# A transformer block on one core: context path at two steps per expert, and three VectorE passes spread over ScalarE and GpSimd

## Chip, core and metric

The kernel runs on one core of a Trainium2 chip. TensorE (PE; its weight loads are PEld), VectorE (DVE), ScalarE (ACT) and GpSimd (POOL) each run their own instructions strictly in order; SyncE (SP) issues the DMAs, also in order; a gather (indirect DMA) is issued by GpSimd. The metric is the device time of one execution in microseconds (us); lower is better.

## Reference, cut to what matters

512 tokens, width 1024, one batch. The first block's attention makes h; then a mixture of 32 experts (two per token), an embedding branch gated by h, and a second block of two attention layers, which also attend to a context of 256 tokens.

```python
def hier_moe(x, w_rg, w_re, w1, w3, w2):
    ...
    def expert_block(args):
        xb, e = args
        hdn = jax.nn.silu(xb @ w1[e]) * (xb @ w3[e])
        return hdn @ w2[e]
    ...
# end of first_block
h = h + hier_moe(rms_norm(h, g_ffn[i]), w_rg[i], w_re[i], w1[i], w3[i], w2[i])
h = h + rms_norm(p[i] @ w_ple[i], g_ple[i]) * jax.nn.sigmoid(rms_norm(h, g_plg[i]) @ w_plg[i])
```

The context goes through the first attention layer of the second block by itself (`yc`, `ctx = ctx + gate_c * yc`) and then gives keys and values (`kc`, `vc`) to the second layer. Nothing of it depends on the experts.

## The kernel before

The program is written out in Python as one long list of instructions. A scheduler puts them in order for each engine: by the order in which the program writes them, moved where its own timing says that an engine would stand idle. So where a filler's instructions stand in the program moves them, but does not fix them.

The part that matters is the loop `for e in range(E)` over the 32 experts (numbered from 0). An expert takes 12 weight tiles `we` of 512 KB (`w1` and `w3` four each, from a ring of 11 tiles `W`; `w2` four, from a ring `Y`), 32 products of `w1` and `w3` (each two instructions, `d<-we,exT`), four transpositions (`t<-ident,eth`), 8 products of `w2` (two instructions each, `d<-we,eth`), and writes its rows to DRAM (`y_d<-ey`). Pairs of experts share a gather `xg` and its transpositions.

Between the experts the loop runs steps of a generator `filler`: first `ctx_path` (56 steps: the keys and values of the context's first layer, four times a projection and two attention pairs, the output product in two halves with 96 products 512 wide `s<-...,cot`, the second layer's input product `mla_in`, and four blocks `mla_kv` whose results are stored as `kvc_d`), then `ple` (a step that loads and transposes the embedding input `px`, and one step for each of four chunks of 128 tokens: 12 products 512 wide, then `pu` is scaled by its norm `r` and by the gain `gple`). `due(e)` says how many steps have to be done after expert e: `CTX_RATE` times e - 1, rounded down. A dense product is done in three fp32r parts (`whi,Xhi`, `wlo,Xhi`, `whi,Xlo`), which need `raw` split into `whi` on ScalarE and `wlo` on GpSimd or VectorE.

Ahead of expert 24 (`OVF_AT`) stands a loop `overflow()` over experts with more than 64 tokens, whose count is a register: all engines meet there. In the profiled execution it has no turn (no instruction touches its tiles `wp`).

Behind the experts every chunk c of 128 tokens gathers its two rows `yk` from `y_d`, adds them to `h2` with the weights `wts`, norms the sum (`row_norm`: squares on ScalarE, then `rsq`: `rs_m` on VectorE, a power on GpSimd), scales it (`xp`), transposes it (`make_X`), and multiplies it by `w_plg` in two blocks of 512 columns, 24 products for a chunk and block (`b_plg`; its tiles are `h2`, `xp`, `pth`). Here it is called the gate product. Nothing of the second block can begin before it.

Of the kernel before, what the change touches and what calls it, by code (L numbers as in the profile page):

```python
# [16 lines left out]
AF = mybir.ActivationFunctionType  # L17
OP = mybir.AluOpType
# [23 lines left out]
PREP_LEAD = 2  # L42
D_PRE, GQA_PRE, MLA_PRE = 5, 14, 34
MOD_FROM, EARLY = 8, 30
CTX_FROM, CTX_RATE, CTX_FINE = 2, 1.65, 3
PREL, OVF_AT, PLE_AT, PLE_FIRST = 2, 24, 29, 2
MLA_ST, MLA_FIRST, MLA_MIX = 2, 8, (1, 3)


# [33 lines left out]
def block_kernel(ctx: ExitStack, tc: tile.TileContext, I, out, dbg=None):  # L83
    nc = tc.nc
# [81 lines left out]
    def share(**us):  # L166

        e = min(us, key=lambda e: held[e] + us[e])
        busy(**{e: us[e]})
        return eng[e]  # L170

    def kcols(ap):
        return math.prod(ap.shape[1:]) / 1000

    def copy(o, i, on=("act", "dve")):

        us = dict(act=0.06 + 0.83 * kcols(o), dve=0.07 + 1.04 * kcols(o))
        e = share(**{n: us[n] for n in on})
        (e.copy if e is nc.scalar else e.tensor_copy)(o, i)  # L179
# [224 lines left out]
    def row_norm(x, n):  # L404

        ssq = SM([P, 1], "ssq1", bufs=4)
        nc.scalar.activation(junk[:, :n], x, AF.Square, accum_out=ssq)
        return rsq(ssq, 1, 1.0 / n)

    def scaled(y, x, r, g):  # L410

        nc.vector.scalar_tensor_tensor(y, x, r, g, op0=OP.mult, op1=OP.mult)
# [591 lines left out]
    for c in range(NC4):  # L1004
        r = row_norm(xs[c], D)
# [466 lines left out]
    xp, gp = [], []  # L1472

    def ple_load():
        if not xp:
            gp.append(Y([P, D], name="gple"))
            gp.append(load_row(gp[0], I["g_ple"], D))
            for c in range(NC4):
                x = T2([P, 256], name="px")
                load(x, I["p"][rows(c), :])  # L1480
                xp.append(x)


    def ple():
        wpv = I["w_ple"].rearrange("(p c) n -> p c n", c=2)
        blks = [Dense(wpv, 2, [(b * 512, 512)]).load().split() for b in range(2)]
        ple_load()
        gp[1]()
        Xp = make_Xs(xp, 2)
        yield  # L1490
        for b, d in enumerate(blks):
            d.X = Xp
            d.evac = lambda c, ps, b=b: copy(us[c][b], ps)
        for c in range(NC4):
            us.append([(K3 if c < 3 else T2)([P, 512], name="pu") for _ in range(2)])
            ssq = SM([P, 2], "ussq")
            for b in range(2):
                blks[b].chunk(c)
                nc.scalar.activation(junk[:, :512], us[c][b], AF.Square, accum_out=ssq[:, b:b + 1])
            nc.vector.tensor_tensor(ssq[:, 0:1], ssq[:, 0:1], ssq[:, 1:2], op=OP.add)  # L1500
            r = rsq(ssq[:, 0:1], 1, 1.0 / D)
            nc.vector.tensor_scalar(r, r, 0.5, None, op0=OP.mult)
            for b in range(2):
                scaled(us[c][b], us[c][b], r, gp[0][:, b * 512:(b + 1) * 512])
            yield

    def due(e):
# [2 lines left out]
    us, paid = [], [0]  # L1510
# [19 lines left out]
    _, wts, yidx, oidx, ovf_e, novf = res  # L1530
# [35 lines left out]
    yks = []  # L1566
# [10 lines left out]
    for c in range(NC4):  # L1577
        h = h2[c]
        if c + 1 < NC4:
            fetch(c + 1)  # L1580
        for k in range(2):
            nc.vector.scalar_tensor_tensor(h, yks[2 * c + k], wts[:, k, c:c + 1], h, op0=OP.mult, op1=OP.add)
        dbg(f"h2_{c}", h)
        r = row_norm(h, D)
        x = Y([P, D], name="xp")
        scaled(x, h, r, gplg)
        Xt.append(make_X(x, 8))
        next(filler, None)
# [356 lines left out]
```

## Time and profile before

| | us |
|---|---|
| median of 3 runs | 1904.56 (1900.89 to 1907.15) |
| the profiled execution: time | 1905.35 |
| its span | 1903.6 |
| TensorE busy | 1682.1 |
| VectorE busy | 932.2 |
| ScalarE busy | 740.0 |
| GpSimd busy | 613.3 |

The span runs from the first to the last instruction of the program; 1.75 us lie around it. Busy times overlap, and a busy TensorE counts the whole latency of a product, so that products which wait for each other look busy. The experts take from 431 to 1052 us of the span, and move 224.6 MB there.

### The profile page before, as it was taken

The numbers are of one execution on the slowest core, as the hardware profiler recorded it, in microseconds if no ns is written. First come the engines' busy times: TensorE is split into PE (matmuls) and PEld (weight loads), VectorE is DVE, ScalarE is ACT, GpSimd is POOL, SyncE is SP. The second block draws the span as 40 slices with busy tenths as digits, with TensorE's granted clock in tenths as the row PEclk, the third lists the DMA queues.
The fourth block names the chain that finished last, engine by engine and source line by source line (L and its number), as shares of the span: only waits on it lengthen the run. The fifth ranks groups of instructions, "written<-read, shape, count | busy, mean of one in ns | idle before, by whom it ended". The sixth has DMA issues, their size and how long they took to land. (4 is left out here: it accounts for less than half of the span.)

```text
span 1903.6 us, 28348 instructions
## 1 busy us (share of the span) xinstructions
PE 1682.1 (88%) x10457; PEld 1202.6 (63%) x10457; DVE 932.2 (49%) x2017; ACT 740.0 (39%) x1620; POOL 613.3 (32%) x697
## 2 busy tenths in 40 slices
PE   7998778969999889899897799898989989879989
PEld 6787555655655545555553478775657877757757
DVE  5765547452232222221233866575652756776641
ACT  5245347412222212221222444355662544656660
POOL 4862113212212212122112434533223545453231
PEclk9999788989999999999898899999999989999999
DMA  8441697778999998998999533100023535331031
GB/s 244 155 173 62 201 283 228 246 259 311 380 409 397 368 380 325 369 322 290 357 409 380 196 105 117 51 1 1 1 89 125 153 108 165 115 98 45 23 133 45
DMA packets 190078, 386.38 MB, mean 203 GB/s; under 512 B 27768, under 2 KB 85720, under 8 KB 189936
## 3 DMA queue, kind: packets, MB, share of 16 engines
q1 hardware_dynamic: 186480, 376.13, 56.2%
q0 software_dynamic: 3456, 8.39, 1.4%
q8 instruction: 84, 1.38, 0.3%
q14 instruction: 58, 0.48, 0.1%
HBM read 350.96 MB, written 39.17 MB: 205 GB/s over the span
## 5 line engine op out<-in xcount | busy, mean ns | idle before, releaser
L150 PE MATMUL d<-we,exT 128*64 128x256 f32 x2048 | 254.9, 393 | 13.2 <-DMA we<-in_w 10.4
L150 PE MATMUL d<-whi,Xhi 128*128 128x512 f32 (+2 forms) x560 | 219.3, 394 | 8.1 <-DVE gsg L588 3.4
L150 PE MATMUL d<-wlo,Xhi 128*128 128x512 f32 (+2 forms) x560 | 218.5, 390 | 3.6 <-POOL wlo L251 3.6
L150 PE MATMUL d<-whi,Xlo 128*128 128x512 f32 (+2 forms) x560 | 218.9, 391 | 2.5 <-DVE Xlo L182 2.4
L251 POOL TENSOR_TENSOR wlo<-raw,whi 128x1024 fp32r<-128x1024 f32 (+2 forms) x71 | 172.5, 2449 | 149.8 <-ACT whi L242 73.8
L150 PEld LDWEIGHTS d<-we,exT 128*64 128x64 f32 x2048 | 149.1, 141 | 102.0 <-issue 22.7
L514 DVE TENSOR_REDUCE ast<-s 128x1 f32<-128x768 f32 (+1 forms) x160 | 135.3, 848 | 99.7 <-PE s L150 97.9
L242 ACT CAST whi<-raw 128x1024 fp32r<-128x1024 f32 (+2 forms) x130 | 131.5, 1019 | 119.6 <-PE d L150 69.2
L516 ACT ACTIVATE pr<-s,ast 128x768 f32<-128x768 f32 (+1 forms) x160 | 131.2, 821 | 59.2 <-DVE ast L514 55.6
L153 PE MATMUL t<-ident,pr 128*128 128x128 f32 x832 | 124.8, 281 | 14.2 <-DVE PT L179 7.0
L150 PE MATMUL s<-stk 128*128 128x256 f32 x448 | 120.4, 355 | 18.7 <-ACT pr L516 14.8
L248 POOL TENSOR_TENSOR wlo<-raw,whi 128x512 fp32r<-128x512 f32 (+2 forms) x69 | 82.1, 1218 | 145.3 <-ACT whi L242 72.0
L150 PEld LDWEIGHTS d<-whi,Xhi 128*128 128x128 f32 x560 | 107.9, 193 | 31.2 <-DVE gsg L588 3.6
L150 PE MATMUL d<-we,eth 128*64 128x512 f32 x512 | 121.8, 606 | 5.2 <-DVE eth L1424 5.2
L150 PEld LDWEIGHTS d<-wlo,Xhi 128*128 128x128 f32 x560 | 108.0, 193 | 24.3 <-POOL wlo L251 4.6
L150 PEld LDWEIGHTS d<-whi,Xlo 128*128 128x128 f32 x560 | 107.8, 192 | 23.5 <-DVE Xlo L182 3.6
L150 PE MATMUL d<-whi,ot 128*128 128x512 f32 x384 | 120.1, 392 | 1.4 <-DVE rT L1283 0.9
L153 PEld LDWEIGHTS t<-ident,pr 128*128 128x128 f32 x832 | 95.7, 143 | 38.3 <-DVE PT L179 11.0
L150 PEld LDWEIGHTS s<-stk 128*128 128x128 f32 x448 | 70.5, 195 | 35.1 <-ACT pr L516 23.6
L1448 POOL DMA_INDIRECT xg<-xn_d,gidx x16 | 16.7, 1041 | 216.8 <-PE t L153 123.4
L1416 DVE SCALAR_TENSOR_TENSOR eth<-eth,d 128x256 f32<-128x256 f32 x32 | 13.5, 421 | 148.4 <-ACT eth L1415 148.4
L150 PEld LDWEIGHTS d<-whi,ot 128*128 128x128 f32 x384 | 71.9, 188 | 18.7 <-issue 1.8
(475 smaller groups left out, 3188.9 us busy)
## 6 DMA issues: line engine op xcount, KB each, us to landing
we<-in_w SPq DMA_DIRECT2D x378, 512.0 KB
raw<-in_l_w_mod SPq DMA_DIRECT2D x48, 512.0 KB
raw<-in_l_w_in SPq DMA_DIRECT2D x64, 256.0 KB
raw<-in_w_in SPq DMA_DIRECT2D x24, 512.0 KB
raw<-in_l_w_out SPq DMA_DIRECT2D x24, 512.0 KB
raw<-in_l_w_in SPq DMA_DIRECT2D x16, 512.0 KB
y_d<-ey SPq DMA_DIRECT2D x64, 128.0 KB
bias<-bias SPq DMA_DIRECT2D x48, 128.0 KB
```

The costliest lines, as they stand in the source:

```text
L150: nc.tensor.matmul(o, l, r, start=start, stop=stop)
L153: nc.tensor.transpose(o, x, identr if x.dtype == F32R else ident)
L242: nc.scalar.copy(t, src)
L248: e.tensor_tensor(t, src[:, k], hi[k].bitcast(F32), op=OP.subtract)
L251: e.tensor_tensor(t, src, whole.bitcast(F32), op=OP.subtract)
L514: nc.vector.tensor_reduce(st[:, h:h + 1], ps, op=OP.max, axis=AX.X, negate=True)
L516: nc.scalar.activation(p, ps, AF.Exp, bias=st[:, h:h + 1], accum_out=sums[:, c, h:h + 1])
L1416: nc.vector.scalar_tensor_tensor(th[:, 256:], th[:, :256], 1.0, ps[:, :256], op0=OP.add, op1=OP.mult)
L1448: nc.gpsimd.indirect_dma_start(out=x, out_offset=None, in_=src, in_offset=bass.IndirectOffsetOnAxis(ap=idx, axis=0), bounds_check=src.shap ...
```

## The change

```diff
-CTX_FROM, CTX_RATE, CTX_FINE = 2, 1.65, 3
-PREL, OVF_AT, PLE_AT, PLE_FIRST = 2, 24, 29, 2
+CTX_FROM, CTX_RATE, CTX_FINE = 2, 2.0, 3
+PREL, OVF_AT, PLE_AT, PLE_FIRST = 2, 24, 28, 2
...
         for b, d in enumerate(blks):
             d.X = Xp
-            d.evac = lambda c, ps, b=b: copy(us[c][b], ps)
+            d.evac = lambda c, ps, b=b: nc.scalar.copy(us[c][b], ps)
...
             for b in range(2):
-                scaled(us[c][b], us[c][b], r, gp[0][:, b * 512:(b + 1) * 512])
+                nc.gpsimd.tensor_tensor(us[c][b], us[c][b], gp[0][:, b * 512:(b + 1) * 512], op=OP.mult)
+                nc.scalar.activation(us[c][b], us[c][b], AF.Copy, scale=r)
...
-        for k in range(2):
-            nc.vector.scalar_tensor_tensor(h, yks[2 * c + k], wts[:, k, c:c + 1], h, op0=OP.mult, op1=OP.add)
+        y0, y1 = yks[2 * c:2 * c + 2]
+        nc.scalar.activation(y0, y0, AF.Copy, scale=wts[:, 0, c:c + 1])
+        nc.gpsimd.tensor_tensor(h, h, y0, op=OP.add)
+        nc.vector.scalar_tensor_tensor(h, y1, wts[:, 1, c:c + 1], h, op0=OP.mult, op1=OP.add)
```

With the rate 2.0 the 56 steps of the context path are due after expert 29, and four more steps (the embedding's first and three of its chunks) after expert 31; with 1.65 there are 49 steps due after expert 31, and the rest stands behind the loop. `PLE_AT` loads the embedding's input one expert earlier. The scaling of `pu` becomes a product on GpSimd and a scaling on ScalarE; the first of the two rows of a token is scaled on ScalarE and added on GpSimd, the second stays on VectorE.

What this does to the order is shown at three places. First SyncE's queue around the overflow loop (`raw<-in_l_w_kv_b` are the weights of `mla_kv`, `raw<-in_w_ple` those of the embedding, `mrow` and `g` small rows). Before, behind the loop:

```order
L129 DMA y_d<-ey 64x512
L129 DMA we<-in_w 128x1024 x16
L129 DMA raw<-in_l_w_kv_b 128x2x512
L129 DMA y_d<-ey 64x512 x2
L129 DMA mrow<-mod_118 1x1024
L129 DMA raw<-in_l_w_kv_b 128x2x512 x2
L129 DMA mrow<-mod_118 1x1024
L129 DMA raw<-in_l_w_kv_b 128x2x512
```

And after the change, in front of the loop (whose first instruction is `COMPARE_AND_BRANCH`):

```order
L129 DMA we<-in_w 128x1024 x6
L129 DMA g_7594<-in_R 1x896
L129 DMA we<-in_w 128x1024 x12
L129 DMA raw<-in_w_ple 128x2x512
L129 DMA y_d<-ey 64x512 x2
L129 DMA we<-in_w 128x1024 x8
L129 DMA y_d<-ey 64x512 x2
L129 DMA we<-in_w 128x1024 x11
L129 DMA raw<-in_w_ple 128x2x512
L129 DMA we<-in_w 128x1024
L129 DMA y_d<-ey 64x512
L1455 COMPARE_AND_BRANCH
```

Four loads for `mla_kv` and both for the embedding have moved from behind the loop to before it.

Second the end of SyncE's queue for the experts, as a piece of the difference (`raw<-in_w_plg` are the weights of the gate product, `h` the tiles `h2`):

```order
+L129 DMA kvc_d<-cvc 128x2x256
+L129 DMA raw<-in_w_plg 128x2x512
+L129 DMA we<-in_w 128x1024
+L129 DMA kvc_d<-cyk 128x2x256
+L129 DMA we<-in_w 128x1024 x6
+L129 DMA y_d<-ey 64x512 x2
+L129 DMA we<-in_w 128x1024 x4
 L129 DMA gplg<-in_g_plg 1x1024
-L129 DMA we<-in_w 128x1024 x3
+L129 DMA h_9180<-h_d 128x1024
+L129 DMA we<-in_w 128x1024
```

The last weight tile, `we` at the end of this piece, now stands behind a load of `w_plg` (three more stand further ahead, not shown) and one of `h2`; before, all loads of `w_plg` and `h2` stood behind the last `we`, as did six of the eight stores `kvc_d`, which now all stand ahead of it.

Third the last part of the experts' tail on GpSimd, from the first gathers `yk`. Before:

```order
L1448 DMA yk<-y_d,yidx 128x1024 x4
L741 TENSOR_TENSOR cyk<-cyk,g_8252 128x256 x2
L196 TENSOR_TENSOR rs_y<-rs_m,mhalf 128x1
L251 TENSOR_TENSOR wlo<-raw,whi 128x1024 x2
L196 TENSOR_TENSOR rs_y<-rs_m,mhalf 128x1 x2
L741 TENSOR_TENSOR cyk<-cyk,g_8252 128x256 x2
L196 TENSOR_TENSOR rs_y<-rs_m,mhalf 128x1
L1448 DMA yk<-y_d,yidx 128x1024 x2
L196 TENSOR_TENSOR rs_y<-rs_m,mhalf 128x1 x2
L1448 DMA yk<-y_d,yidx 128x1024 x2
L196 TENSOR_TENSOR rs_y<-rs_m,mhalf 128x1 x2
```

After:

```order
L1448 DMA yk<-y_d,yidx 128x1024 x4
L1584 TENSOR_TENSOR h_9180<-h_9180,yk 128x1024
L1584 TENSOR_TENSOR h_9181<-h_9181,yk 128x1024
L196 TENSOR_TENSOR rs_y<-rs_m,mhalf 128x1
L1504 TENSOR_TENSOR pu<-pu,gple 128x512
L1448 DMA yk<-y_d,yidx 128x1024 x2
L1504 TENSOR_TENSOR pu<-pu,gple 128x512
L196 TENSOR_TENSOR rs_y<-rs_m,mhalf 128x1 x2
L1448 DMA yk<-y_d,yidx 128x1024 x2
L1584 TENSOR_TENSOR h_9182<-h_9182,yk 128x1024
L1584 TENSOR_TENSOR h_9183<-h_9183,yk 128x1024
L196 TENSOR_TENSOR rs_y<-rs_m,mhalf 128x1 x2
```

The two splittings `wlo` and the context's last `cyk` are gone from here, and four additions and two products stand in their place. On VectorE, behind the last expert's copy, after the change (`h_9180` to `h_9183` are the four chunks, `t_9432` is the second chunk's transposition):

```order
L412 SCALAR_TENSOR_TENSOR xp<-h_9181,rs_y,gplg 128x1024
L1585 SCALAR_TENSOR_TENSOR h_9182<-yk,wts,h_9182 128x1024
L1585 SCALAR_TENSOR_TENSOR h_9183<-yk,wts,h_9183 128x1024
L194 TENSOR_SCALAR rs_m<-ssq_9457 128x1
L1604 SCALAR_TENSOR_TENSOR pth<-pth,pu 128x512
L182 TENSOR_TENSOR Xlo<-t_9432,Xhi 128x512
L182 TENSOR_TENSOR Xlo<-t_9439,Xhi 128x512
L412 SCALAR_TENSOR_TENSOR xp<-h_9182,rs_y,gplg 128x1024
```

The second chunk's `Xlo`, which the gate product of that chunk needs, stands behind the sums of the third and the fourth chunk.

## Rows read from the trace of the kernel before

**Rows 1.** Windows at experts 4, 13, 24: engines' busy us, clock, DMA share, GB/s

```profile
496.00:670.00 174.00, 161.67 (x1082) 97.77 (x1081) 46.08 (x131) 44.34 (x108) 41.16 (x48) 1.00 1.01 389
670.00:893.00 223.00, 200.43 (x1297) 118.28 (x1296) 49.90 (x127) 49.14 (x119) 46.67 (x51) 0.96 0.92 340
893.00:1052.00 159.00, 136.96 (x837) 75.57 (x836) 47.84 (x117) 34.69 (x73) 29.73 (x26) 0.90 0.98 374
1052.00:1101.00 49.00, 35.09 (x150) 26.27 (x150) 43.81 (x88) 25.18 (x57) 23.35 (x22) 0.90 0.47 156
```

**Rows 2.** Timeline, TensorE: one expert's parts, then two dense products

```profile
877.47 3.67 PE L150 MATMUL d<-we,exT 128*64 128x256 f32 x32
893.96 3.65 PE L150 MATMUL d<-we,eth 128*64 128x512 f32 x16
1030.10 0.66 PE L153 MATMUL t<-ident,eth 128*64 128x128 f32 x4
1110.01 0.39 PE L150 MATMUL d<-whi,Xlo 128*128 128x512 f32 x1
1110.24 0.39 PE L150 MATMUL d<-whi,Xhi 128*128 128x512 f32 x1
```

**Rows 3.** Waits of SyncE's queue in 520:640, 640:880, 960:1040: total, times, longest

```profile
SPq L129 <- DMA we<-in_w: 57.1, 68, 1.5
SPq L129 <- PE d L150: 88.4, 88, 4.5
SPq L129 <- DMA we<-in_w: 41.6, 50, 1.4
```

**Rows 4.** Timeline, SyncE: at the overflow loop; the last weights' issue

```profile
883.82 9.75 SPq L129 DMA_DIRECT2D y_d<-ey  x2
893.63 15.07 SPq L129 DMA_DIRECT2D we<-in_w  x16
1025.11 1.87 SPq L129 DMA_DIRECT2D we<-in_w  x3
```

**Rows 5.** Timeline, TensorE: from the last expert to the gate product

```profile
1037.11 2.76 PE L150 MATMUL d<-we,exT 128*64 128x256 f32 x24
1045.69 5.84 PE L150 MATMUL d<-we,eth 128*64 128x512 f32 x16
1080.54 1.94 PE L153 MATMUL t<-ident,xp 128*128 128x128 f32 x8 [9.49 <-DVE rs_y L1502]
1100.10 0.71 PE L153 MATMUL t<-ident,xp 128*128 128x128 f32 x4 [0.89 <-DVE Xlo L182]
```

**Rows 6.** Timeline, 1056 to 1081: GpSimd (two rows), VectorE (three rows)

```profile
1056.56 1.04 POOL L1448 DMA_INDIRECT yk<-y_d,yidx  x1 [9.49 <-PE s L150]
1069.68 5.76 POOL L251 TENSOR_TENSOR wlo<-raw,whi 128x1024 fp32r<-128x1024 f32 x2 [6.00 <-PE d L150]
1066.18 0.15 DVE L201 SCALAR_TENSOR_TENSOR rs_u<-rs_m,rs_y 128x8 f32<-128x8 f32 x1
1070.97 2.19 DVE L203 SCALAR_TENSOR_TENSOR rs_y<-rs_u,rs_y 128x8 f32<-128x8 f32 x1
1079.13 1.27 DVE L412 SCALAR_TENSOR_TENSOR xp<-h,rs_y,gplg 128x1024 f32<-128x1024 f32 x1
```

**Rows 7.** Tile yk: the sums on VectorE, and the gathers' landing

```profile
L1582 DVE SCALAR_TENSOR_TENSOR h<-yk,wts,h x8: 1269/1278/1285, 1063.1 to 1092.5; 128x1024 f32<-128x1024 f32 x8
DMA to landing us min/median/max: 4.5/6.7/7.1
```

**Rows 8.** Groups by form (busy us, mean ns): GpSimd's splittings

```profile
L251 POOL TENSOR_TENSOR wlo<-raw,whi 128x1024 fp32r<-128x1024 f32 x65 | 162.5, 2519 | 136.9 <-PE d L150 67.3 <-ACT whi L242 60.9 <-DMA raw<-in_w_out 6.6
L248 POOL TENSOR_TENSOR wlo<-raw,whi 128x512 fp32r<-128x512 f32 x54 | 68.4, 1297 | 119.5 <-ACT whi L242 62.6 <-issue 32.3 <-DMA we<-in_w 16.2
```

**Rows 9.** Tile pu: VectorE's scaling, ScalarE's copies (ns min/median/max)

```profile
L412 DVE SCALAR_TENSOR_TENSOR pu<-pu,rs_y,gple x8: 739/748/1291, 1068.3 to 1086.6; 128x512 f32<-128x512 f32 x8
L179 ACT COPY pu<-d x4: 564/576/589, 1058.6 to 1072.1; 128x512 f32<-128x512 f32 x4
```

## The prediction

> **What bounds the kernel now.** I read the windows first, cut where the first product of an expert begins. From expert 4 to 13 (496 to 670 us) the DMA engines are full (share 1.01); from 13 to 24 they fall to 0.92 and 340 GB/s; from 24 to the end of the last expert they are at 0.98; then, up to the steady part of the gate product, at 0.47, and TensorE is busy for 35 of 49 us [rows 1]. In this last stretch VectorE has 43.8 of 49 us: there it is the full engine. The waits of SyncE's queue say the same: between 520 and 640 us it waits for earlier weights to land (57 us), between 640 and 880 mostly for TensorE to give tiles back (88 us), between 960 and 1040 for the landing again (42 us) [rows 3]. So the experts are bound by the DMAs, then by TensorE, then by the DMAs.
>
> Busy TensorE counts latency, so I price its work from runs of products. 32 instructions of w1 and w3 take 3.67 us, so 7.3 for the 64; w2 takes 3.65; the four transpositions 0.66 [rows 2]; with half a pair's gathered rows (about 0.5, an estimate from these four) an expert is 12.2 us. A dense product 512 wide is issued every 0.23 us [rows 2]. With half of this for 256 wide, and 0.13 (estimated) for a transposition, I counted the filler's work in both orders: what stands ahead of the experts 4, 13, the overflow loop, and the last w2 is 14, 62, 114, 133 us before, and 17, 63, 128, 146 us after.
>
> **The experts up to the overflow loop.** 14 us of TensorE work and 4.2 MB of loads (four for mla_kv, two for the embedding, two weight tiles) move from behind the loop to before it. Up to expert 13 the two counts agree within 3 us, so I take no difference there. From 13 to the loop TensorE has 11 x 12.2 + 52 = 186 us of work in 223, that is 83%; after the change 11 x 12.2 + 65 = 199. The 4.2 MB have room: at the 389 GB/s of the stretch before, the 223 us would carry 11 MB more than at 340 [rows 1]. What 14 us of work cost depends on whether the idle 17% can be used. From 4 to 13 the same engine did 9 x 12.2 + 48 = 158 us in 174, or 91%; at that share 199 us take 219, 4 us less than now. If every idle moment stays, the loop comes 14 us later. I take +5, the middle of -4 and +14: the earlier stretch is the nearest row, but this one holds the coarser steps (the output product's halves, 11 us each).
>
> **From the loop to the last weights.** SyncE stands at the loop (9.75 us for two stores), begins again at 893.6, and issues the last weight tile at about 1027 [rows 4]: 133 us. In the order before, 52.3 MB go out in between; after, 52.6 MB: four loads of w_plg, one of h2 and six stores of the context come ahead of the last weights, and what moved before the loop makes room for them. At 389 GB/s 52.6 MB take 135 us, at the 374 of the whole stretch 141 [rows 1]; this stretch already ran at 393. So it can hardly give more than the few us in which the second layer's context products keep TensorE from freeing tiles, and these now lie before the loop. I take -3, between 0 and -5.
>
> **The last expert.** Its w1 and w3 end at 1039.9; its w2 runs from 1045.7 to 1051.5 [rows 5], 5.84 us where 3.65 are normal [rows 2]: the granted clock is 0.90 on the mean of this stretch [rows 1], so part of it is at 1.2 instead of 2.4 GHz. After the change two of the embedding's chunks (24 products, 5.5 us) stand between them in place of the gain's broadcast. They fill the wait and keep TensorE at work, but lie in front of w2. I take -1 (0 to -2).
>
> **The tail.** Times from here on count from the end of w2 (1051.5). Before, the first gather starts at +5.1 [rows 6], the first sum at +11.6 [rows 7], the first xp only at +27.6 [rows 6], its transposition at +29.1, after 9.5 us of idle, and TensorE is steady from +49 on, with two chunks done and the third begun (50 dense products lie between) [rows 5].
>
> The arithmetic that leaves VectorE here: four sums of 1.28 [rows 7], eight scalings of 0.75 and four copies, which take ScalarE 0.58 [rows 9] and VectorE hardly less, some 13 us in all, most of the scalings and copies now within the experts. GpSimd gets four additions of 128x1024 and eight products of 128x512; the trace has none of these, and the nearest rows are its splittings of the same shape with two inputs, 2.5 and 1.3 us [rows 8]. ScalarE's scaling of 1024 columns I put at 1.1, twice a copy of 512 [rows 9]. So a chunk's sum, once 2.6 us on one engine, becomes 1.1 + 2.5 + 1.3 on three. I walk along the new order: first rows at +10 (a landing takes 4.5 to 7.1 us [rows 7]), scaled at +11, added at +13.6, second row at +15; the next chunk's rows land at about +14.5, its addition ends at +18; the first chunk's power stands behind it on GpSimd, +18.7; xp ends at +21, and the gate product may begin at +23.5 instead of +31.
>
> But the second chunk's Xlo now stands on VectorE behind the sums of the third and fourth. Their gathers stand on GpSimd behind two products and three powers: the last first-row gather goes out at about +25, lands at +32, is scaled and added by +35; VectorE's sum ends at +36.5, Xlo at +38. TensorE is steady from +38, with one chunk done and the second begun: behind the old state by one chunk (24 x 0.23 = 5.5) and 12 transpositions (1.6). 49 - 38 - 7 is a gain of 4 us (0 to 6).
>
> One row speaks against this part. A VectorE operation on 8 columns took 2.19 us, begun while GpSimd was in two splittings of 5.76 [rows 6]; one of that shape just before it took 0.15 [rows 6]. I take 1.2 us off the walk for one such stop of xp behind a product of pu; this is in the 4. The Trainium skill (SBUF — State Buffer, section "SBUF: two separate sides") says that GpSimd and a VectorE operation with two SBUF inputs share a port pair that one of them holds for a whole instruction. By that rule, the trace agrees: that operation has two such inputs. Were each of the six GpSimd operations to stop VectorE for its full length (4 x 2.5 + 2 x 1.3 = 12.6), the gain would be gone; most of the time VectorE waits for these very results, so I leave that to a rival.
>
> **Sum.** +5 - 3 - 1 - 4 = -3 us on the profiled execution's 1905.4, so 1902.4; the median stands 0.8 lower. I predict 1902. Behind the gate product both orders differ only by a few exchanged transpositions and products (some 70 of 2,400 rows on TensorE), for which I allow 2 us. About 0.3% (5.7 us) is what a measurement of this kernel can tell from no change.
>
> **Rivals.** *The idle time before the loop is used* (30%): the stretch from 13 to 24 runs as densely as the one before it. For it: the DMA share there is lower only because TensorE holds tiles [rows 3], and the new order spreads the output product's halves. Against it: TensorE's latency chains are as many as before. The loop comes no later (0), the rest gives -4, -1, -5: 1895.
> *The moved work is paid in full* (20%, slower): before the loop TensorE is what SyncE waits for [rows 3], so 14 us of work push the loop back by 14; behind it the DMAs are full and give nothing, -0 - 1 - 3: +10, 1915. It decides from a loop more than 11 us later, if the tail gives no more than 4.
> *The tail is not shortened* (12%): the gathers' landing and the port hold the sums, as worked out; +5 - 3 - 1 + 0: 1906.
> The change could fail to do what it says only in the tail's order, which is read above.
>
> **Chances.** My forecast has 38%: 30 within 0.3%, 7 faster, 1 slower. The first rival (30) is faster, the second (20) slower; of the third, 10 are within, 2 slower. Faster 0.37, same 0.40, slower 0.23. The range takes in the first rival with a denser tail (1890) and the second but for its far end (1914); the forecast's own is 1897 to 1908.
>
> **What would show it.** The last issue ahead of the overflow loop and SyncE's restart: near 899 if I am right, 907 or more for the second rival, 893 or less for the first. From there to the last weight tile 128 to 133 us. The first transposition of xp at 22 to 24 us behind the last w2 instead of 29, and a wait of TensorE for Xlo in the second chunk. An addition on GpSimd much above 2.5 us, or a VectorE operation of over 2 us beside one, speaks for the third rival. I am wrong if the loop's place moves by more than 10 us either way, or if the first stretch, where I took no difference, is not the same.

## The result and the profile after

The changed kernel takes 1936.08 us (median of 4 runs, 1930.59 to 1940.74), the kernel before 1902.72 us beside it (4 runs, 1899.51 to 1907.15). The ratio is 1.0164, 95% interval 1.0138 to 1.0191: 33 us slower, outside my range, which ended at 1914. (One run of a kernel below, 2013.5 us at a granted clock of 0.815 where its nine others took 1909 to 1921, is left out.) The profiled execution of the changed kernel has a span of 1930.9 us, 27.3 more than that of before; the terms below are made against this one.

The windows of the changed kernel, cut again where experts 4, 13 and 24 begin and where the last w2 ends (same columns as [rows 1]):

```profile
496.00:670.00 174.00, 160.99 (x1075) 100.51 (x1073) 48.27 (x137) 43.21 (x112) 37.33 (x46) 0.95 0.97 364
670.00:930.00 260.00, 223.89 (x1390) 138.48 (x1388) 66.42 (x174) 62.79 (x144) 58.06 (x62) 0.90 0.86 324
930.00:1079.00 149.00, 130.77 (x794) 69.84 (x791) 34.80 (x101) 35.34 (x77) 26.87 (x23) 0.93 0.97 378
1079.00:1130.00 51.00, 23.38 (x87) 17.83 (x85) 17.36 (x25) 19.80 (x32) 31.25 (x21) 0.67 0.38 129
```

Beside [rows 1]: the first stretch is as long as it was (174 us), the second 37 us longer (260 for 223) with emptier DMAs (324 GB/s for 340) and a lower granted clock (0.90 for 0.96), the third 10 us shorter (149 for 159). In the last, VectorE has gone from 43.8 of 49 us to 17.4 of 51, and nothing was won by it. SyncE's queue at the overflow loop and at the last weight tile, which answers to [rows 4]:

```profile
916.01 12.33 SPq L129 DMA_DIRECT2D y_d<-ey  x2
...
929.03 3.71 SPq L129 DMA_DIRECT2D we<-in_w  x6
...
1056.53 1.11 SPq L129 DMA_DIRECT2D we<-in_w  x1
```

The queue stands at the loop at 916 instead of 884 and goes on with weights at 929.0 instead of 893.6: 35.4 us later. From there to the end of the last weight issue it needs 128.6 us, where it was about 133. TensorE's timeline from the last w2 on, which answers to [rows 5]:

```profile
1074.99 3.65 PE L150 MATMUL d<-we,eth 128*64 128x512 f32 x16
...
1081.20 0.39 PE L150 MATMUL d<-whi,Xlo 128*128 128x512 f32 x1
1102.12 1.97 PE L153 MATMUL t<-ident,xp 128*128 128x128 f32 x8 [20.53 <-DVE xp L412]
...
1117.42 0.80 PE L150 MATMUL d<-whi,Xhi 128*128 128x512 f32 x1 [4.90 <-ACT Xhi L390]
...
1120.44 0.80 PE L150 MATMUL d<-whi,Xlo 128*128 128x512 f32 x1 [1.79 <-DVE Xlo L182]
```

The last w2 now takes 3.65 us instead of 5.84 and ends at 1078.6. The first transposition of xp comes 23.5 us later (29.0 before; I had 22 to 24), but after 20.5 us of idle in one piece, and the second chunk waits for its Xhi and Xlo as foreseen: TensorE is steady from +42, where I had +38.

### The profile page after: what moved, and what is told of

The parts are those of the page before. It is cut to its first block, busy times and chain, and to the rows that moved or that the text cites. A ratio compares the mean times of both kernels' runs of the same rounds, so it can differ in the third digit from the quotient of the medians.

```text
span 1930.9 us, 28369 instructions
## 1 busy us (share of the span) xinstructions
PE 1686.3 (87%) x10457; PEld 1213.0 (63%) x10457; DVE 918.3 (48%) x1999; ACT 753.7 (39%) x1638; POOL 633.4 (33%) x709
## 5 line engine op out<-in xcount | busy, mean ns | idle before, releaser
L150 PE MATMUL d<-whi,Xhi 128*128 128x512 f32 (+2 forms) x560 | 219.6, 394 | 11.1 <-ACT Xhi L390 5.6
L150 PE MATMUL s<-whi,Xhi 128*128 128x512 f32 (+2 forms) x192 | 76.4, 401 | 5.6 <-ACT pr L516 4.2
```

The costliest lines, as they stand in the source:

```text
L150: nc.tensor.matmul(o, l, r, start=start, stop=stop)
```

## What the experiments share

All times by stretch below are read from the timelines in the same way: from the start of the span to the first product of expert 13, from there to the first of expert 24, from there to the end of the last w2, and the rest. They and the spans are those of the profiled execution; the medians are over all runs of a kernel, and a span is about 2 us shorter than its own execution's time. Ratios are against runs of the kernel before that were made beside each (medians 1901.8 to 1903.5). The first lines are the two kernels.

```
                                to e13   13-24   24-w2 end   behind    span    median
before                           670.1   222.9     158.5     852.0   1903.6   1902.7
changed                          670.4   259.3     148.9     852.3   1930.9   1936.1
rate alone                       674.3   259.6     149.8     841.2   1924.9   1926.1
sharing alone, rate 1.65         669.9   223.2     156.9     870.3   1920.3   1925.3
rate 2.0, four experts later     654.7   249.9     156.0     848.5   1909.1   1914.8
rate 1.8                         690.2   255.0     141.7     847.4   1934.2   1939.3
3 steps each behind the loop     670.2   224.2     175.3     831.3   1900.9   1903.1
sums alone shared                671.1   223.5     155.5     850.8   1900.9   1904.6
scalings alone shared            670.5   223.3     154.9     862.2   1910.9   1913.9
rate 2.0, shifted by one step    679.9   248.6     153.1     842.1   1923.7   1926.0
one projection's products twice  672.8   229.8     154.2     848.6   1905.4   1907.0
early staging, rate 2.0          673.2   246.6     149.4     833.2   1902.4   1907.4
early staging, rate 1.65         669.1   225.3     158.4     846.2   1899.0   1899.2
rate 1.5                         657.8   229.7     143.5     867.6   1898.5   1900.7
changed, additions on VectorE    675.2   259.2     148.0     847.7   1930.1   1931.5
changed, scalings put back       676.4   260.1     150.7     840.5   1927.7   1924.8
early staging, rate 1.8          690.3   249.5     138.9     851.5   1930.2   1932.5
early staging, 3 behind loop     663.1   223.3     175.4     838.9   1900.7   1912.3
```

For the stretch from 13 to 24 TensorE's time is split further. The interval from one instruction's start to the next counts as work where it is no longer than 2.3 times the usual one for its kind (0.115 us for a product of w1 or w3, 0.228 for w2 and dense ones, 0.13 for a transposition); where it is longer, the excess over the usual one is a wait. Work and waits add up to the stretch within 0.8 us:

```
                                 13-24    work   waits
before                           222.9   183.2    39.4
changed                          259.3   202.2    56.9
rate alone                       259.6   202.3    56.8
rate 2.0, four experts later     249.9   197.6    51.7
rate 1.8                         255.0   192.1    62.4
rate 2.0, shifted by one step    248.6   196.3    52.0
one projection's products twice  229.8   197.7    31.9
early staging, rate 2.0          246.6   200.1    45.7
```

So the 36.4 us of the changed kernel are 19.0 of work (dense products +14.4, their number from 144 to 216; broadcasts of rows +3.2; the second layer's transpositions +3.6; the others -2.2) and 17.5 of waits. Two things are mixed in. Part of the added work is the same work at a lower clock: the granted clocks of 0.96 and 0.90 mean some 18 and 52 us at 1.2 instead of 2.4 GHz, and about 7 and 21 us of the work fell into them, so up to 7 of the 19 us (an estimate from these figures; at half speed an interval is still below 2.3 times the usual one). And by the instruction that TensorE has to wait with, some 10 us of the added waits stand ahead of the steps' own instructions, and some 7 ahead of the experts', of which 5.3 are one wait at the overflow loop, where all engines meet. TensorE's wait there before and in the changed kernel (total, times, longest):

```profile
PE t L153 <- SPq L1455: 3.0, 1, 3.0
```

```profile
PE t L153 <- SPq L1455: 8.3, 1, 8.3
```

The profile of the changed kernel names no wait of TensorE for a weight tile in this stretch. My theory from here on is that the steps' place costs the time, since each step brings waits of its own to an engine that works in order (a step is a chain over several engines: products, a copy, a splitting, transpositions, each waiting for the one before); the rival is that the sharing, or the order that comes of it, costs it.

## Which half of the change costs it

**Rate alone.** Sums and scalings as before.

```
-CTX_FROM, CTX_RATE, CTX_FINE = 2, 1.65, 3
-PREL, OVF_AT, PLE_AT, PLE_FIRST = 2, 24, 29, 2
+CTX_FROM, CTX_RATE, CTX_FINE = 2, 2.0, 3
+PREL, OVF_AT, PLE_AT, PLE_FIRST = 2, 24, 28, 2
```

> The kernel before with the two numbers of the change alone: a rate of 2.0 steps for each expert and the embedding's loads at expert 28; the sums and scalings stay on VectorE. First theory (the steps' place costs the time): SyncE stops at the overflow loop about 35 us later than before, as in the changed kernel, and the experts behind it give about 9 us back; the time is between 1928 and 1938 us. Rival (the work given to ScalarE and GpSimd, or the order that the planner of engines makes of it, costs the time): the loop stays where it was within 5 us, and the time is between 1898 and 1908 us. If both count, it lies between.

Measured 1926.07 us, ratio 1.0123 (1.0086 to 1.016): 24 us slower, just below the 1928 to 1938 of the theory and far above its rival's. The stretch from 13 to 24 is that of the changed kernel, to 0.3 us. But behind the last w2 this kernel is 11 us shorter than before (841.2), which the changed one is not (852.3).

**Sharing alone.** The changed kernel with the old rate.

```
-CTX_FROM, CTX_RATE, CTX_FINE = 2, 2.0, 3
-PREL, OVF_AT, PLE_AT, PLE_FIRST = 2, 24, 28, 2
+CTX_FROM, CTX_RATE, CTX_FINE = 2, 1.65, 3
+PREL, OVF_AT, PLE_AT, PLE_FIRST = 2, 24, 29, 2
```

> The changed kernel with the rate put back to 1.65 and the embedding's loads to expert 29; the sums and scalings stay shared with ScalarE and GpSimd. First theory (the steps' place costs the time): the experts run as before, and only the tail can differ; in the changed kernel the tail from the end of the last w2 on was as long as before within 1 us, so 1898 to 1906 us. Rival (the sharing costs the time): 1925 us or more. The tail alone: the first transposition of xp 22 to 25 us after the last w2 instead of 29, but the steady part of the gate product no earlier than 4 us less.

Measured 1925.34 us, ratio 1.0116 (1.0083 to 1.0149). By my theory there should have been no difference; the rival's 1925 or more came out. The experts run as before (223.2), and everything is lost behind the last w2 (870.3 for 852.0): the first transposition of xp comes at +35.5 instead of +29.0, the last at +65.7 instead of +52.2. So both halves cost, in different places, and neither theory alone is right. GpSimd's timeline of this kernel shows where:

```profile
1059.16 1.00 POOL L1448 DMA_INDIRECT yk<-y_d,yidx  x1 [0.30 <-ACT junk L1499]
...
1061.57 2.52 POOL L1504 TENSOR_TENSOR pu<-pu,gple 128x512 f32<-128x512 f32 x2
...
1065.00 2.36 POOL L1584 TENSOR_TENSOR h<-h,yk 128x1024 f32<-128x1024 f32 x1
...
1073.21 2.33 POOL L1584 TENSOR_TENSOR h<-h,yk 128x1024 f32<-128x1024 f32 x1
1075.51 4.63 POOL L251 TENSOR_TENSOR wlo<-raw,whi 128x1024 fp32r<-128x1024 f32 x2
...
1081.61 2.48 POOL L1504 TENSOR_TENSOR pu<-pu,gple 128x512 f32<-128x512 f32 x2
1084.05 1.72 POOL L196 TENSOR_TENSOR rs_y<-rs_m,mhalf 128x1 f32<-128x1 f32 x2
1085.74 2.51 POOL L1504 TENSOR_TENSOR pu<-pu,gple 128x512 f32<-128x512 f32 x2
1088.40 1.87 POOL L1448 DMA_INDIRECT yk<-y_d,yidx  x1
```

Between the second pair of gathers (the last at 1059.16) and the third (1088.40) GpSimd is hardly ever idle: eight products, two additions and two splittings stand in its queue, and the gathers of the third and fourth chunk behind them.

**Sums alone, and scalings alone, at the old rate.** The first has the four lines of the combine loop, the second the three of the embedding (both as in the change's diff).

> The kernel before with the sums alone shared (ScalarE scales, GpSimd adds, VectorE does the second half). The two sharings together cost 18 us behind the last w2 in the run above. If GpSimd's four additions of 128x1024 are what costs (each stands for 2.3 us ahead of the gathers in its queue, and a chunk's sum becomes a chain over three engines): 1912 to 1925 us, and the last first-row gather starts 5 us or more later than before (33.9 us after the last w2). If the eight products of the scalings are what holds the gathers: 1899 to 1907 us.

> The kernel before with the embedding's copies on ScalarE and its scalings on GpSimd and ScalarE; the sums stay on VectorE. If GpSimd's eight products of 128x512 (1.3 us each, six of them between the first and the third pair of gathers in its queue) hold the gathers: 1912 to 1925 us. If the sums are what costs: 1899 to 1907 us. If either delays them only together with the other, both kernels stay below 1910 us.

Sums: 1904.57 us, ratio 1.002 (1.0005 to 1.0036). Scalings: 1913.87 us, ratio 1.0067 (1.0046 to 1.0087). By the time it is the scalings; together the two cost more (23 us) than one by one (2 and 11). By the profiled executions it is both: the last transposition of xp comes at +57.2 with the sums alone and at +58.2 with the scalings alone, 5 and 6 us later than before, and the kernel with the sums alone takes 7 us back between the residuals of the two layers, where nothing was edited. So it is not shown that the sums cost nothing at this rate. With the sums alone the third pair's first gather starts 32.5 us behind the last w2. With the scalings alone it starts at 36.5 (27.6 before), with eight products, 10.7 us in all, between it and the second pair.

**The same at the changed rate.** The changed kernel, once with the additions on VectorE, once with the scalings put back.

```
-        nc.gpsimd.tensor_tensor(h, h, y0, op=OP.add)
+        nc.vector.tensor_tensor(h, h, y0, op=OP.add)
```

```
-                nc.gpsimd.tensor_tensor(us[c][b], us[c][b], gp[0][:, b * 512:(b + 1) * 512], op=OP.mult)
-                nc.scalar.activation(us[c][b], us[c][b], AF.Copy, scale=r)
+                scaled(us[c][b], us[c][b], r, gp[0][:, b * 512:(b + 1) * 512])
```

(In the second the copies go back too, to `copy(us[c][b], ps)`.)

> The changed kernel with its four additions of the sums on VectorE instead of GpSimd (ScalarE still scales the first row, the scalings stay shared). If GpSimd's additions (2.3 to 3.3 us each, and the gathers behind them in its queue) make up most of the 10 us by which the changed kernel is above the rate alone: 1924 to 1930 us, and the last transposition of xp falls from 55 us behind the last w2 to 50 or less. If it is the scalings' products: 1932 to 1940 us.

> The changed kernel with the embedding's copies and scalings as before (VectorE), the sums still shared. If the scalings on GpSimd and ScalarE make up most of the 10 us: 1924 to 1930 us, last transposition of xp at 50 us or less behind the last w2. If it is the sums: 1932 to 1940 us.

Additions on VectorE: 1931.45 us, ratio 1.015 (1.0128 to 1.0171), between the 1924 to 1930 that would have put the loss on them and the 1932 to 1940 of the scalings; last transposition of xp at +52.0 (changed: +55.0). Scalings put back: 1924.77 us, ratio 1.0118 (1.0097 to 1.0139), last transposition at +46.3, and as fast as the rate alone. So of the 33 us of the change some 23 are the rate, and taking the scalings out gives 11 back (1936.1 less 1924.8). At this rate the sums cost nothing where the scalings are not shared (1924.8 for 1926.1), but 4.6 us beside them (1936.1 less 1931.5). GpSimd's timeline of the changed kernel shows how few operations stand ahead of the gathers:

```profile
1095.21 3.33 POOL L1584 TENSOR_TENSOR h<-h,yk 128x1024 f32<-128x1024 f32 x1 [0.19 <-ACT yk L1583]
1098.50 0.57 POOL L196 TENSOR_TENSOR rs_y<-rs_m,mhalf 128x1 f32<-128x1 f32 x1
1099.05 1.93 POOL L1504 TENSOR_TENSOR pu<-pu,gple 128x512 f32<-128x512 f32 x1
1101.15 1.85 POOL L1448 DMA_INDIRECT yk<-y_d,yidx  x1 [0.17 <-issue]
1103.30 0.99 POOL L1448 DMA_INDIRECT yk<-y_d,yidx  x1 [0.30 <-issue]
1104.31 1.30 POOL L1504 TENSOR_TENSOR pu<-pu,gple 128x512 f32<-128x512 f32 x1
1105.55 1.10 POOL L196 TENSOR_TENSOR rs_y<-rs_m,mhalf 128x1 f32<-128x1 f32 x2
1106.82 2.08 POOL L1448 DMA_INDIRECT yk<-y_d,yidx  x1 [0.17 <-POOL rs_y L196]
```

Two additions (the second is the first line) and one product stand between the second and the third pair of gathers, and one more product ahead of the fourth. The fourth pair starts 28.2 us behind the last w2; with the scalings put back, where the two additions still stand, it is 23.6, and with the rate alone 22.6:

```profile
1099.92 1.56 POOL L196 TENSOR_TENSOR rs_y<-rs_m,mhalf 128x1 f32<-128x1 f32 x1 [4.90 <-DVE rs_m L194]
1101.66 2.05 POOL L1448 DMA_INDIRECT yk<-y_d,yidx  x1 [0.18 <-issue]
...
1106.31 1.21 POOL L1448 DMA_INDIRECT yk<-y_d,yidx  x1 [0.18 <-issue]
```

(The last w2 ends at 1083.7 there.) That the products cost by their place in this queue is read from these timelines. In the runs the copies and scalings on ScalarE went back together with the products, so no run has the products alone.

## What the rate costs, and why

**The same work ahead of the loop, in denser steps.** Two steps per expert, begun four experts later.

```
+CTX_FROM, CTX_RATE, CTX_FINE = 6, 2.0, 3
```

> The kernel before with two steps for each expert, but begun four experts later: ahead of the overflow loop stands the same work as before (115 us of TensorE by my count; 128 in the changed kernel), while between expert 13 and the loop the steps come as densely as in the changed kernel. If what counts is the amount ahead of the loop, the loop comes within 8 us of before, and the time is 1898 to 1912 us. If what counts is the two steps that go with every expert (TensorE stands in one step's chains while the next expert's weights wait for tiles), the stretch from 13 to 24 takes 250 us or more as in the changed kernel instead of 223; the experts from 4 to 10, which now have less to do, can give some of it back; the time is then 1910 us or more.

Measured 1914.84 us, ratio 1.0061 (1.0039 to 1.0082). The stretch from 13 to 24 takes 249.9 us, 27 more than before: work +14.4, waits +12.3. Ahead of it 15 us are given back. So it is what stands in this stretch that costs, not the sum ahead of the loop.

**A rate between the two**, 1.8 (embedding's loads at 29).

> The kernel before with a rate of 1.8; ahead of the overflow loop stand 124 us of the steps' work, two thirds of the way from before (115) to the changed kernel (128). If the time follows the amount of work ahead of the loop, the loop comes 20 to 27 us later and the time is 1914 to 1928 us. If the loss of the changed kernel belongs to single meetings of its order (the 44 us of expert 13, the stores at the loop), there is no such proportion: 1900 to 1908 us or over 1930 us are as likely.

Measured 1939.28 us, ratio 1.0197 (1.016 to 1.0235): slower than 2.0 with less work moved. The loss does not follow the amount. From 4 to 13 this kernel loses 23 us at somewhat less work than before (149.6 us for 153.3), by waits of 46.7 for 20.2 us, of which 21.3 stand ahead of the transpositions of staged q and k (3.8 before).

**The pairs shifted by one step** at 2.0.

```
+CTX_FROM, CTX_RATE, CTX_FINE = 2.5, 2.0, 3
```

> The kernel with the changed rate alone, two steps for each expert, but the pairs shifted by one step: one less in all ahead of every expert, another pairing of a projection with the attention behind it. If the cost lies in the work and the waits of the steps themselves, whichever are paired: 1918 to 1932 us, as with the rate alone (1926). If it lies in single pairs (a projection and the attention that needs it with no expert between), the time moves by more than 8 us from 1926 to either side, and the wait of TensorE for the staging tile changes by as much.

Measured 1925.99 us, ratio 1.0127 (1.0107 to 1.0148), the time of the rate alone. From 4 to 13 it is 6 us slower, from 13 to 24 11 us faster: another pairing moves the waits, their sum hardly. At this rate the loss is not the luck of one pairing.

**Work without a chain.** The kernel before, with the 48 products of one projection done twice, the first pass thrown away.

```
-            for k in range(nk):
+            for k in [*range(nk)] * (1 + self.more):
...
+            blk.more = int(hk == 3)
```

> The kernel before, in which the third head group's projection (the fourth of four) does its 48 products of 512 columns twice, the first pass into the same bank and thrown away: 11 us more work for TensorE between expert 16 and 18, no new chain, load or wait. If TensorE's idle time there can be used, as the prediction took for the most part, the overflow loop stays within 4 us: 1899 to 1907 us. If work is paid in full there: loop 9 to 14 us later, 1909 to 1919 us. If more than in full (weight tiles come back late as well, and the clock falls): loop 16 us or more later, 1918 us or more.

Measured 1907.03 us, ratio 1.0022 (1.0006 to 1.0038). The loop comes 9.6 us later, of which 2.7 lie ahead of expert 13, where nothing was changed; the stretch grows by 6.9 us at 14.5 more of work, and its waits fall from 39.4 to 31.9. The loop's place is in the range of work paid in full, the time at the upper end of that of idle time used. So products alone do use some of the idle time, as the prediction hoped: 11 us cost 7 in the stretch and 4 at the end. The 13 us that I had counted for the moved steps cost 36 in the same stretch.

**The chain begun earlier.** At the rate 2.0 the first splitting of q and k of each head group is done in the projection's step.

```
-            yield from block(blk, done)
...
+            prep, *rest = pair(0)
...
+                for f in prep:
+                    if f.__name__ == "stage":
+                        f()
...
+            yield from block(blk, done_and_stage)
+            prep = [f for f in prep if f.__name__ != "stage"]
+            yield from group_steps([lambda prep=prep, rest=rest: (prep, *rest), lambda: pair(1)])
```

> The kernel with the changed rate alone, but a head group's first staging (the splitting of q and k, for which TensorE waited 21.5 us in ten places ahead of the loop) is done in the projection's step and no longer in the attention's first step. If the waits of the steps' chains are half of what the rate cost (17.5 of 36 us, as the count of TensorE's gaps says), this wait falls below 12 us, the loop comes 8 to 18 us earlier than 934, and the time is 1908 to 1920 us. If TensorE then only waits for something else, the loop and the time stay: 1921 to 1931 us.

Measured 1907.38 us, ratio to before 1.0031 (1.0013 to 1.0049), 19 us less than the rate alone and just below the 1908 to 1920 expected. The loop comes 14 us earlier (919.8 for 933.9); the waits in the stretch fall by 11.1 us and the work by 2.2. No work was left out, so this run shows that the place of a step's chain costs time: 13 of the 36 us come back. Another 8 come behind the last w2 (833.2 for 841.2), 7 of them between the residuals of the two layers; these are not explained by the staging. TensorE's timeline from expert 13's products on in the changed kernel (the rate alone has the same waits, of 3.49 and 2.36 us), and then with the early staging:

```profile
679.33 0.50 PE L150 MATMUL s<-stk 128*128 128x256 f32 x2
683.32 0.36 PE L153 MATMUL t<-identr,stg 128*128 128x128 f32 x2 [3.49 <-POOL stg L189]
686.18 0.49 PE L153 MATMUL t<-identr,stg 128*128 128x128 f32 x2 [2.50 <-POOL stg L189]
...
690.44 5.97 PE L150 MATMUL d<-we,eth 128*64 128x512 f32 x16 [1.03 <-DVE eth L1424]
...
714.37 1.95 PE L150 MATMUL d<-we,exT 128*64 128x256 f32 x16
```

```profile
677.45 1.08 PE L150 MATMUL d<-we,exT 128*64 128x256 f32 x8
678.46 0.51 PE L150 MATMUL s<-stk 128*128 128x256 f32 x2
678.90 1.08 PE L150 MATMUL d<-we,exT 128*64 128x256 f32 x8
680.31 0.37 PE L153 MATMUL t<-identr,stg 128*128 128x128 f32 x2 [0.33 <-POOL stg L189]
680.60 1.08 PE L150 MATMUL d<-we,exT 128*64 128x256 f32 x8
...
685.67 3.65 PE L150 MATMUL d<-we,eth 128*64 128x512 f32 x16
...
707.31 1.95 PE L150 MATMUL d<-we,exT 128*64 128x256 f32 x16
```

In the first, expert 13's products are done at 679.4, ahead of the rest of the attention's chain; TensorE stands for 3.49 and 2.50 us at staging tiles, expert 12's w2 behind it takes 5.97 us instead of 3.65 (the granted clock between 680 and 700 us is 0.74, with the early staging 1.00), and the next expert begins at 714.4, 44.0 us after the one before. In the second the same transpositions lie between pieces of eight products of the expert and wait 0.33 us, w2 takes 3.65, and the next expert begins at 707.3, after 34.2 us. What SyncE waits for meanwhile, in the changed kernel between 640 and 780 us (columns as in [rows 3]):

```profile
SPq L129 <- PE d L150: 42.4, 36, 13.3
...
SPq L129 <- PE t L153: 15.9, 3, 12.5
```

Single waits of 13.3 and 12.5 us for TensorE (4.5 and 4.0 before): for this long no new weight tile is asked for.

The waits by name fall by less than the 11 us. From 496 to 930 us, in the changed kernel and then with the early staging, TensorE's waits for staging tiles:

```profile
PE t L153 <- POOL stg L189: 21.5, 10, 5.5
```

```profile
PE t L153 <- POOL stg L189: 15.9, 9, 5.4
```

That is 5.6 us less (I had expected a fall below 12); the other half of the 11 is a wait ahead of w2, 6.7 before and 0.6 us after by my count.

**Early staging at the old rate, and at 1.8.**

> The same earlier staging in the kernel before, at its own rate. The wait for the staging tile is 13.8 us in nine places there. If such waits are on the path: 1890 to 1898 us, faster than both kernels. If they are covered by the DMAs at this rate: 1899 to 1906 us.

> A rate of 1.8, which was the slowest (1939 us; TensorE waited 32.8 us for staging tiles ahead of the loop), with the staging done in the projection's step. If waits in the steps' own chains are what sets the order of the rates: the wait falls by 10 us or more and the time to 1903 to 1920 us. If another thing makes this rate slow: 1928 to 1940 us.

At 1.65: 1899.22 us, ratio 0.9977 (0.9963 to 0.9991), 4 us faster than before and the fastest version of the study; the staging wait falls from 13.8 to 10.3 us. The gain lies below the 1890 to 1898 of waits on the path, in the range of waits covered by the DMAs, and by the stretches behind the last w2 (846.2 for 852.0), not at the loop: 6 us less between the residuals of the two layers. Where it comes from is not settled. At 1.8: 1932.53 us, ratio 1.0153 (1.0133 to 1.0173), 7 us less than 1.8 without it, and the wait does not fall at all. From 494 to 690 us, at 1.8 and at 1.8 with the early staging:

```profile
PE t L153 <- POOL stg L189: 19.7, 7, 5.6
```

```profile
PE t L153 <- POOL stg L189: 20.9, 8, 5.5
```

So up to expert 13 this wait is the largest part of what 1.8 loses, and the earlier step does not take it away there: the result of the rate 2.0 does not carry over. I suppose that projection and attention then stand behind the same expert; it was not tried.

## Behind the loop

**Three steps per expert behind the loop, the old rate ahead of it.**

```
-        return int(CTX_RATE * max(0, e + 1 - CTX_FROM)) - paid[0]
+        n = int(CTX_RATE * max(0, min(e, OVF_AT - 1) + 1 - CTX_FROM)) + 3 * max(0, e + 1 - OVF_AT)
+        return n - paid[0]
```

> The kernel before with its rate of 1.65 up to the overflow loop and three steps for each expert behind it, so that the embedding's first chunks stand among the last experts as in the changed kernel; sums and scalings stay on VectorE. Theory (up to the loop TensorE sets the pace and every moved step costs its work and its own waits there; behind it the DMAs do): the loop stands where it was (893 us within 4), the stretch from expert 24 to the end of the last w2 grows by less than 8 us over the 158 of before, and the part behind that w2 is 7 to 11 us shorter, as with the changed rate alone (841 instead of 852): 1890 to 1902 us. Rival (a moved step costs wherever it stands): 16 us more work among the last eight experts brings 16 to 35 us there, and the time is 1906 to 1928 us.

Measured 1903.07 us, ratio 0.9997 (0.9982 to 1.0012). (The embedding's loads stand at 28 here.) The loop stays (894.4), the stretch behind it grows by 16.8 us, and behind the last w2 20.7 us are given back in the profiled execution. The theory had less than 8 for the stretch: a step costs behind the loop too, although the DMAs were full there. About 7 of the 20.7 lie up to the last transposition of xp (+45.3 for +52.2), and 10.6 between the residuals of the two layers, where neither edit nor order was meant to change anything.

**Both together**: the early staging with this.

> The earlier staging at 1.65 (1899 us, the fastest so far) with three steps for each expert behind the overflow loop, which alone came out as before (1903: 17 us more among the last experts, and as much less behind them). If the two add up: 1896 to 1902 us, no clear gain over the earlier staging alone. If the waits that early staging removes are also those of the second layer's steps behind the loop: 1888 to 1896 us.

Measured 1912.3 us, ratio 1.0057 (1.0036 to 1.0078), its runs between 1902.5 and 1920.8; the profiled one is the fastest of them and shows no loss. I had expected 1888 to 1902, so neither reading holds, and why the other runs are slower is open.

**The shift made the other way**, a rate of 1.5.

> The kernel before with a rate of 1.5: 104 us of the steps' work ahead of the overflow loop instead of 115, so the change's shift made the other way round. By the price that the changed rate showed (14 us of work moved ahead of the loop cost 36 there, and gave 9 among the last experts and 11 behind them), 11 us moved back give 11 to 28 at the loop and cost 8 to 16 behind it: 1888 to 1902 us. If the changed rate's loss belongs to its own order and not to the amount: 1900 to 1915 us.

Measured 1900.7 us, ratio 0.999 (0.9976 to 1.0004): no difference, a time that both readings allowed. Ahead of expert 13 it wins 12 us, up to the last w2 20.5, and gives 15.6 back behind it, where the steps now stand. The stretch from 13 to 24 is 6.8 us longer than before with no more steps in it, so which steps stand there counts as well as how many. The price of the changed rate does not come back the other way.

## Why the prediction was wrong

**The step that failed** is the +5 for the loop, "the middle of -4 and +14". It asked only whether 14 us of work can use TensorE's idle 17%. The doubled projection shows that bare products can, in part. But most of the idle time (some 24 of the 39 us of waits, sorted by instruction as above) already stood ahead of the steps' own instructions, and more steps brought more of it: the stretch grew by 36.4 us, of which 19.0 is work (I had counted 13, without the broadcasts, the second layer's transpositions and the lower clock) and 17.5 waits, 5.3 of these at the overflow loop. Even the second rival, "the moved work is paid in full", which named the right side, was less than half of it, and at 1915 it lay just outside a range that was meant to take it in.

**From the loop to the last weights** -3 was right by its own measure: 128.6 us where 133 stood, within 0 to -5. **The last expert** -1 was right as well: from its first product to the end of its w2 24.7 us where it was 25.5, with w2 at 3.65 us. From the last weight issue to the end of the last w2 it is 21.0 us where it was 24.5, more than the term had; the whole stretch is 9.6 us shorter, where the two terms had 4. Why this part is shorter is not shown.

**The tail** -4 came out at +0.2. The first transposition of xp (23.5 us) and the wait for Xlo came as foreseen, but the walk that led there was 2 to 3 us short at every step: the first addition began at +14.0 and not at +11, xp was done at +23.4 and not at +21. The shorter tail is there (the rate alone gives -10.8), but by the steps' place, and the shared scalings take it back. I had walked that order and put the fourth first-row gather at +25; it went out at +28.2. The third rival (12%) had the effect, by the landing and the port; what the timelines show is the products ahead of the gathers in GpSimd's queue, and 2.7 us at the port (below).

**Up to expert 13** no difference was right for the changed kernel (+0.3 us), though the steps there cost 23 us at the rate 1.8.

**What stays open.** From the first layer's residual to the second's, which no edit touches, the kernels of the study take between 440 and 453 us (450.6 before), so up to 13 us between two of them can come from there, and what sets them is open. How a rate of 1.8 comes to its waits, and whether the wait ahead of w2 that goes with the staging at 2.0 is part of the same chain, is not settled either.

## What to carry to other kernels

TensorE's idle time took in part of the work that had no chain of its own (11 us of products cost 7) and nothing of the steps that have one (13 us by my count cost 36). Price a moved step by its work and by the waits that such steps already have in that stretch: here 39.4 us of waits stood beside some 52 of the steps' work, so that 19 more of work would have brought about 14 of waits, 33 in all, where 36 was measured. This rule is made from the run that it explains. Of the others it fits the two with 2.0 and another pairing (11 and 10 for 12.3 and 12.6 us of waits) and fails at 1.8 (7 for 23.0) and with the early staging (13 for 6.3), so it is a first guess and no more. And before an operation goes to an engine that has time, look at what else that engine issues: with two products of 1.9 and 1.3 us ahead of them on GpSimd, the fourth chunk's gathers left at 28.2 us behind the last w2 instead of 23.6 (scalings put back, ScalarE's part too), and its xp was transposed at 55.0 instead of 46.3.

## What was not expected of the hardware

After an idle stretch of 20.5 us TensorE's products come at half speed. In the changed kernel, just behind the first transpositions of xp and some microseconds later:

```profile
1104.50 0.63 PE L150 MATMUL d<-wlo,Xhi 128*128 128x512 f32 x1
1104.93 0.63 PE L150 MATMUL d<-whi,Xlo 128*128 128x512 f32 x1
...
1110.79 0.39 PE L150 MATMUL d<-whi,Xhi 128*128 128x512 f32 x1
1111.02 0.39 PE L150 MATMUL d<-wlo,Xhi 128*128 128x512 f32 x1
```

They start 0.43 us apart, then 0.23, that is at 1.2 and 2.4 GHz; the granted clock between 1102 and 1107 us is 0.50, and in the window from 1079 to 1130 it is 0.67 (0.90 in [rows 1]). So the wait also costs the first products behind it, 0.2 us each for some ten here. Before, behind 9.5 us of idle, it was four or five. Whether one long wait costs more than many short ones is not shown: TensorE is also idle for longer in all.

GpSimd is slowed by VectorE as VectorE is by GpSimd. In the changed kernel the addition begun at 1095.21 took 3.33 us where the others take 2.34 to 2.38, and the product begun at 1099.05 1.93 us instead of 1.28. VectorE's timeline beside them:

```profile
1095.05 1.28 DVE L1585 SCALAR_TENSOR_TENSOR h<-yk,wts,h 128x1024 f32<-128x1024 f32 x1 [15.66 <-POOL h L1584]
...
1098.57 1.28 DVE L1585 SCALAR_TENSOR_TENSOR h<-yk,wts,h 128x1024 f32<-128x1024 f32 x1 [0.81 <-POOL h L1584]
1099.77 2.29 DVE L412 SCALAR_TENSOR_TENSOR xp<-h,rs_y,gplg 128x1024 f32<-128x1024 f32 x1
```

When the addition began, VectorE's sum had 1.12 us to go, and the addition took 1.0 longer; when the product began, the next sum had 0.80 to go, and the product took 0.65 longer; when xp began, the product had 1.21 to go, and xp took 1.0 longer. The Trainium skill (SBUF — State Buffer, section "SBUF: two separate sides") has GpSimd and a VectorE operation with two SBUF inputs, as these sums and xp are, share a port pair that one of them holds for a whole instruction; the trace agrees with this in both directions. It is 2.7 us in all here.
